# Two feed-forward products: 512-column inner products, and output sums kept in PSUM

## Chip, cores and metric

The kernel runs on one core of a Trainium2 chip. The metric is the device time of one execution in microseconds (us). In three runs the kernel before took 989.38, 989.68 and 989.70 us; 989.68 is the median.

## What is computed

The reference is one transformer layer on 512 tokens of width 1024, all in float32:

```
h = x
h = h + 0.5 * swiglu(rmsnorm(h, ffn1_norm), ffn1_w_in, ffn1_w_out)
h = h + hybrid_mixer(rmsnorm(h, mix_norm), ...)       # attention, not touched by the change
h = h + 0.5 * swiglu(rmsnorm(h, ffn2_norm), ffn2_w_in, ffn2_w_out)
out = rmsnorm(h, final_norm)

def swiglu(x, w_in, w_out):            # w_in: 1024 x 5632, w_out: 2816 x 1024
    gate, up = jnp.split(x @ w_in, 2, axis=-1)
    return (jax.nn.silu(gate) * up) @ w_out
```

The change lies in the two feed-forward parts (FFN 1 and FFN 2).

## The kernel before

**Layout.** Activations lie transposed, 128 rows of the width on the partitions and the 512 tokens along the free dimension; `h` holds eight such slices. Every float32 operand `a` of a matmul is split into a high part (rounded to the fp32r format by a ScalarE copy) and a low part (the rest, by a VectorE subtraction). A product `w x` is then three matmuls: `w_high x_high`, `w_high x_low`, `w_low x_high`.

**FFN by blocks.** The 2816 gate columns and 2816 up columns make 22 blocks of 128 + 128. Blocks 0 to 2 are plain: eight steps of three 512-column matmuls for gate and for up (lines 217 to 219). Blocks 3 to 21, the inner blocks, use a 2 x 2 scheme with seven products in place of eight: `x` is cut into upper and lower half of the width and into tokens 0 to 255 (`t1`) and 256 to 511 (`t2`), and sums of those quarters (`sums_of_x`, once per FFN) are multiplied by sums of the quarters of the weights (`sums_of_w`, once per block: lines 320 to 341). Each product has four steps of three 256-column matmuls (`product`, lines 352 to 354).

**The seven products of a block j** are issued in the order 1, (4 of block j-1), 5, 6, 2, 3, 7; 4 follows behind product 1 of the next block. Product 1 goes to `b1` (PSUM pool `sc`) and is copied to `b2` (one of two fixed banks in pool `mm`) by line 575; product 5 goes to `b3` (pool `mm`) and is copied out by line 582; product 6 adds to `b2`, and line 585 writes `b3 = b2 + su`; product 2 adds to `b1` (gate of `t1`: lines 588, 589); product 3 adds to `b3`; product 7 adds to `b2` (lines 594 to 596); product 4 adds to `b2` (gate of `t2`: lines 599, 600). `finish` (606) multiplies gate and up, and `put_g` (372, 374) splits the result. `bc` is the norm's factor, spread over all partitions.

**Output steps.** Blocks form groups that end at 2, 6, 10, 14, 18 and 22. When a group is finished, `out_steps` multiplies it by `w_out` for each of the eight slices i of `h`: the weights are split by lines 404 and 405, then 512-column matmuls (217 to 219) go into a fresh `sc` bank, and line 427, on VectorE, adds half of it to `h[i]`. These steps are spread between the inner products by `out_advance`, which pays out a budget of time after each product. The last group runs alone, in FFN 1 through `out_steps` and in FFN 2 through `out_last`.

**What sets the order.** The program states an order and a scheduler decides how each engine's queue is filled; each engine then works its own queue strictly in that order, and waits for semaphores where an operand comes from another engine. PSUM has eight banks: pool `mm` four, `sc` three, `pv` one.

Of the kernel before, what the change touches and what calls it, by code (L numbers as in the profile page):

```python
# [12 lines left out]
AF = mybir.ActivationFunctionType  # L13
ALU = mybir.AluOpType
AX = mybir.AxisListType

P = 128
T = 512
D = 1024
KB = D // P  # L20
# [13 lines left out]
ENDS = [2, 6, 10, 14, 18, 22]  # L34
# [10 lines left out]
def tile_hybrid(ctx, tc, xT, f1_wi, f1_wo, wm_t, wm_n, cw1, cw2, small, wm_oa, wm_ob, wm_oc, f2_wi, f2_wo, const, out):  # L45
# [6 lines left out]
    def f(ap):  # L52
        return ap.bitcast(F32)

    def ps(tag="mm"):
        return psp.tile([P, 512], F32, tag=tag, name=tag, bufs=NB[tag])
# [4 lines left out]
    def ps_any():  # L61
        turn[0] += 1
        return ps(wide_ps[turn[0] % 5])

    def flat(dt=F32R):
        return sb.tile([P, 1024], dt, tag="u", name="u", bufs=NU)
# [7 lines left out]
    def tmp():  # L74
        return sb.tile([P, 512], F32, tag="tmp", name="tmp", bufs=NTMP)
# [45 lines left out]
    def split_next():  # L121
        if not loaded:
            load_next()
        if loaded:
            raw, n, whole = loaded.pop(0)
            if whole:
                split.append(raw)
            else:
                wh, wl = flat(), flat()
                to_parts(raw, wh, wl, slice(0, n))  # L130
                split.append((wh, wl))
            load_next()
# [49 lines left out]
    def feed(k, gcol, xs, acc):  # L182
        parts(k, gcol, xs)
        squares(k, acc)
# [27 lines left out]
    def mm3_steps(o, wh, wl, ks, xs, first, last):  # L212
        for q, k in ks:
            c = slice(q * P, (q + 1) * P)
            s0 = first and k == ks[0][1]
            s1 = last and k == ks[-1][1]
            PE.matmul(o, wh[:, c], xs[k][:, 0, :], start=s0, stop=False)  # L217
            PE.matmul(o, wh[:, c], xs[k][:, 1, :], start=False, stop=False)  # L218
            PE.matmul(o, wl[:, c], xs[k][:, 0, :], start=False, stop=s1)  # L219
            yield 0.65  # L220

    def run(gen):
        for _ in gen:
            pass
# [7 lines left out]
    def sums_of_x(xs, gcol, XF):  # L232

        t1, t2 = slice(0, 256), slice(256, 512)
        xg = [None] * 4

        def scaled(*us):
            for u in us:
                t = xg[u] = unit(F32)
                for a in range(2):  # L240
                    k = 2 * u + a
                    gc = sm[:, gcol + k : gcol + k + 1]
                    if gcol == S_G2 and u % 2 == 0:
                        V.tensor_scalar(t[:, a, :], h[:, k, :], gc, None, op0=ALU.mult)
                    else:
                        A.activation(t[:, a, :], h[:, k, :], AF.Copy, scale=gc)

        def sums(kp, n):
            a, b = xg[kp], xg[2 + kp]
            s = flat(F32).rearrange("p (s k t) -> p s k t", s=2, k=2)  # L250
            if n == 0:
                V.tensor_tensor(s[:, 0], a[:, :, t2], b[:, :, t2], op=ALU.add)
                V.tensor_tensor(s[:, 1], s[:, 0], a[:, :, t1], op=ALU.subtract)
                s2[kp] = s[:, 1]
            else:
                V.tensor_tensor(s[:, 0], a[:, :, t1], a[:, :, t2], op=ALU.subtract)
                V.tensor_tensor(s[:, 1], b[:, :, t1], s2[kp], op=ALU.subtract)
            return s

        def high(s):  # L260
            sh = flat().rearrange("p (s k t) -> p s k t", s=2, k=2)
            A.copy(sh, s)
            return sh

        def low(s, sh, n):
            sl = flat().rearrange("p (s k t) -> p s k t", s=2, k=2)
            V.tensor_tensor(sl, s, f(sh), op=ALU.subtract)
            for m in range(2):
                XF["S", 2 * n + m + 1].extend((sh[:, m, k], sl[:, m, k]) for k in range(2))


        s2 = [None] * 2
        scaled(0)
        yield
        scaled(2)
        yield
        sa = sums(0, 0)
        yield
        scaled(1)
        sb_ = sums(0, 1)  # L280
        ha = high(sa)
        yield
        scaled(3)
        low(sa, ha, 0)
        yield
        hb = high(sb_)
        sc = sums(1, 0)
        yield
        low(sb_, hb, 1)
        sd = sums(1, 1)  # L290
        hc = high(sc)
        yield
        low(sc, hc, 0)
        hd = high(sd)
        yield
        low(sd, hd, 1)
        yield
        for name, ks, t in (("A11", 0, t1), ("A12", 4, t1), ("A22", 4, t2)):
            XF[name].extend((xs[k][:, 0, t], xs[k][:, 1, t]) for k in range(ks, ks + 4))

    def load_raw(wi, j):
        t = double()
# [43 lines left out]

    def product(o, w, x, first):

        for k in range(4):
            c = slice(k * P, (k + 1) * P)  # L350
            new = first and k == 0
            PE.matmul(o, w[0][:, c], x[k][0], start=new, stop=False, skip_group_check=not first)  # L352
            PE.matmul(o, w[0][:, c], x[k][1], start=False, stop=False, skip_group_check=not first)  # L353
            PE.matmul(o, w[1][:, c], x[k][0], start=False, stop=k == 3, skip_group_check=not first)  # L354

    def ffn(xs, acc, wi, wo, plain, gnext):

# [2 lines left out]
        bc = rcol = None  # L360
# [6 lines left out]
        nxs = []  # L367
# [50 lines left out]
            return w  # L418

        def out_steps(g):  # L420
            j0, j1 = starts[g], ENDS[g]
            last = g == len(ENDS) - 1
            for i in range(KB):
                wh, wl = out_w()
                o = ps_any() if last else ps("sc")
                yield from mm3_steps(o, wh, wl, [(q, j0 + q) for q in range(j1 - j0)], gs, True, True)
                V.scalar_tensor_tensor(h[:, i, :], o, 0.5, h[:, i, :], op0=ALU.mult, op1=ALU.add)  # L427
                if last:
                    feed(i, gnext, nxs, nacc)
                    if i == KB // 2:  # L430
                        split_next()

        def out_last():

# [63 lines left out]
        def side_step(n=1):  # L498
            for _ in range(n):
                while side and next(side[0], side) is side:  # L500
                    side.pop(0)
# [22 lines left out]
        for n in range(2 * plain):  # L524
# [30 lines left out]
            while bc is not None and held:  # L555
                gated(*held.pop(0))
        side_step(20)
        outs.append(out_steps(0))


        t1, t2 = slice(0, 256), slice(256, 512)

        banks = [ps()[:, t1] for _ in range(2)]
        for o in banks:
            PE.matmul(o, xs[0][:, 0, :P], xs[0][:, 0, t1], start=True, stop=True)

        live = {}
        later = []

        def piece_of(j, p):  # L570
            if p == 1:
                live[j] = ps("sc")[:, t1], banks[j % 2], None, None, None
                b1, b2 = live[j][:2]
                product(b1, WF.pop((j, "B11")), XF["A11"], True)
                A.copy(b2, b1)
                return
            b1, b2, b3, su, z = live[j]
            if p == 5:
                b3, su, z = ps()[:, t1], tmp(), tmp()
                live[j] = b1, b2, b3, su, z  # L580
                product(b3, WF.pop((j, "T1")), XF["S", 1], True)
                A.copy(su[:, t1], b3)
            elif p == 6:
                product(b2, WF.pop((j, "T2")), XF["S", 2], False)
                V.tensor_tensor(b3, b2, su[:, t1], op=ALU.add)
            elif p == 2:
                product(b1, WF.pop((j, "B21")), XF["A12"], False)
                V.tensor_tensor(z[:, t1], b1, bc[:, t1], op=ALU.mult)
                A.activation(z[:, t1], z[:, t1], AF.Silu)
            elif p == 3:  # L590
                product(b3, WF.pop((j, "B22")), XF["S", 4], False)
            elif p == 7:
                product(b2, WF.pop((j, "T3")), XF["S", 3], False)
                V.tensor_tensor(su[:, t2], b2, su[:, t1], op=ALU.add)
                V.tensor_tensor(su[:, t1], b3, bc[:, t1], op=ALU.mult)
                V.tensor_tensor(su[:, t2], su[:, t2], bc[:, t2], op=ALU.mult)
            elif p == 4:
                product(b2, WF.pop((j, "T4")), XF["A22"], False)
                V.tensor_tensor(z[:, t2], b2, bc[:, t2], op=ALU.mult)
                A.activation(z[:, t2], z[:, t2], AF.Silu)  # L600
                del live[j]
                later.append(finish(j, su, z))

        def finish(j, su, z):
            gg = tmp()
            V.tensor_tensor(gg, su, z, op=ALU.mult)
            yield from put_g(j, gg)

        order = []
        for j in range(plain, FB):  # L610
# [23 lines left out]
        if gnext is None:  # L634
            out_last()
        else:
            run(out_steps(len(ENDS) - 1))
        return nxs, nacc

    def last_norm(t0, sacc, sq):  # L640
# [723 lines left out]
```

## Time and profile before

| | |
|---|---|
| median of three runs | 989.68 us |
| the profiled execution | 989.41 us |
| its span, first to last instruction | 987.5 us |
| PE busy | 972.7 us |
| DVE busy | 799.8 us |
| ACT busy | 507.2 us |

PE is TensorE, PEld its weight loads, DVE VectorE, ACT ScalarE. The span is 1.9 us shorter than the execution's time. Matmuls overlap in the array, so the "mean ns" of a matmul is longer than the time at which the next one follows; what a matmul costs is the distance between the starts of two neighbours. "Idle" in a row is time of that engine alone, and costs nothing where another engine is the bottleneck.

### The profile page before, as it was taken

The page shows a single profiled execution, that of the slowest core. Times are in us where ns is not written, and L with a number is a line of the kernel's source. Part 1 is how long each engine was busy: PE and PEld are TensorE (multiplying, and loading weights), DVE is VectorE, ACT ScalarE, POOL GpSimd, SP SyncE. Part 2 cuts the span into 40 slices and gives each one's busy share as a digit, 9 for nine tenths or more (in the row PEclk, how much of TensorE's full clock was granted, in tenths as well). Part 3 has the DMA queues.
Part 4 walks back from the last instruction along what each step waited for, and adds up shares of the span by engine and source line. Part 5 has one row for each costly group of instructions (what it writes and reads, how often), then busy time and mean ns, then how long its engine had stood idle before and what let it go on. Part 6 is the DMA issues. An engine that isn't in the chain of part 4 may idle for free.

```text
span 987.5 us, 15987 instructions
## 1 busy us (share of the span) xinstructions
PE 972.7 (98%) x6228; PEld 870.4 (88%) x6228; DVE 799.8 (81%) x1459; ACT 507.2 (51%) x1037; POOL 3.8 (0%) x7
## 2 busy tenths in 40 slices
PE   9999999999999999999999999999999999999997
PEld 7889999999999889888777878889999999999996
DVE  6999788787796575788799989999978878789664
ACT  8655344353444355554678776745434435344354
POOL 0000000000000000000000000000000000000000
PEclk9999999999999999999999999999999999999999
DMA  8142413233124313123310212224231322412112
GB/s 313 44 154 102 150 44 139 76 107 131 62 86 144 125 43 106 43 71 107 130 43 8 79 44 75 86 70 162 82 136 52 130 84 99 149 44 97 45 42 86
DMA packets 36075, 93.61 MB, mean 95 GB/s; under 512 B 4384, under 2 KB 8864, under 8 KB 36000
## 3 DMA queue, kind: packets, MB, share of 16 engines
q1 hardware_dynamic: 36000, 92.59, 27.1%
q8 instruction: 49, 0.80, 0.3%
q14 instruction: 26, 0.21, 0.1%
HBM read 88.87 MB, written 2.10 MB: 92 GB/s over the span
## 4 chain that ended last, share of the span: by engine, by line
PE 91%; DVE 5%; ACT 2%; issue 1%; DMA 1%; POOL 0%; SPq 0%; DVEq 0%; ACTq 0%
PE mm L353 9%; PE mm L352 9%; PE mm L354 9%; PE sc L217 8%; PE sc L219 8%; PE sc L218 8%; PE mm L217 4%; PE mm L219 4%; PE mm L218 4%; PE sc L353 3%; PE sc L354 3%; PE sc L352 3%; PE mm L936 2%; PE pv L973 2%; PE pv L974 2%; PE mm L792 1%
## 5 line engine op out<-in xcount | busy, mean ns | idle before, releaser
L354 PE MATMUL mm<-u 128*128 128x256 f32 x760 | 214.7, 283 | 0.0
L352 PE MATMUL mm<-u 128*128 128x256 f32 x760 | 214.4, 282 | 0.3 <-ACT u L328 0.3
L353 PE MATMUL mm<-u 128*128 128x256 f32 x760 | 214.6, 282 | 0.0
L352 PEld LDWEIGHTS mm<-u 128*128 128x128 f32 x760 | 144.5, 190 | 7.7 <-ACT u L328 0.5
L353 PEld LDWEIGHTS mm<-u 128*128 128x128 f32 x760 | 144.8, 191 | 5.5
L217 PE MATMUL sc<-u 128*128 128x512 f32 x364 | 144.3, 396 | 2.3 <-ACT u L404 2.1
L354 PEld LDWEIGHTS mm<-u 128*128 128x128 f32 x760 | 144.8, 191 | 0.5
L218 PE MATMUL sc<-u 128*128 128x512 f32 x364 | 143.6, 395 | 0.0
L219 PE MATMUL sc<-u 128*128 128x512 f32 x364 | 142.7, 393 | 0.0
L217 PE MATMUL mm<-u 128*128 128x512 f32 x220 | 89.8, 408 | 0.0
L219 PE MATMUL mm<-u 128*128 128x512 f32 x220 | 86.9, 395 | 0.0
L218 PE MATMUL mm<-u 128*128 128x512 f32 x220 | 86.5, 393 | 0.0
L354 PE MATMUL sc<-u 128*128 128x256 f32 x304 | 86.0, 283 | 0.3 <-DVE u L325 0.3
L353 PE MATMUL sc<-u 128*128 128x256 f32 x304 | 85.9, 283 | 0.0
L352 PE MATMUL sc<-u 128*128 128x256 f32 x304 | 85.7, 282 | 0.0
L219 PEld LDWEIGHTS sc<-u 128*128 128x128 f32 x364 | 68.4, 188 | 17.6 <-DVE u L405 1.8
L217 PEld LDWEIGHTS sc<-u 128*128 128x128 f32 x364 | 69.2, 190 | 9.7 <-ACT u L404 2.5
L404 ACT CAST u<-tmp 128x512 fp32r<-128x512 f32 (+1 forms) x96 | 55.0, 583 | 44.2 <-PE sc L219 21.0
L218 PEld LDWEIGHTS sc<-u 128*128 128x128 f32 x364 | 69.2, 190 | 6.3
L427 DVE SCALAR_TENSOR_TENSOR h<-sc,h 128x512 f32<-128x512 f32 x85 | 58.3, 686 | 11.7 <-PE sc L219 11.6
L405 DVE TENSOR_TENSOR u<-tmp,u 128x512 fp32r<-128x512 f32 (+1 forms) x96 | 60.8, 640 | 8.2 <-ACT u L404 8.0
L352 PEld LDWEIGHTS sc<-u 128*128 128x128 f32 x304 | 57.9, 190 | 2.6
(255 smaller groups left out, 2033.7 us busy)
## 6 DMA issues: line engine op xcount, KB each, us to landing
t<-in_f_wi_dram SPq DMA_DIRECT2D x88, 512.0 KB, 4.5
tmp<-in_f_wo_dram SPq DMA_DIRECT2D x80, 256.0 KB, 4.8
t<-in_wm_t_dram SPq DMA_DIRECT2D x13, 512.0 KB, 3.8
t<-in_cw_dram SPq DMA_DIRECT2D x8, 512.0 KB, 4.5
h<-in_xT_dram SPq DMA_DIRECT2D x4, 512.0 KB, 7.4
tmp<-in_f_wo_dram SPq DMA_DIRECT2D x16, 128.0 KB, 4.6
t<-in_wm_oa_dram SPq DMA_DIRECT2D x4, 512.0 KB, 4.1
out_dram<-tmp SPq DMA_DIRECT2D x8, 256.0 KB, 2.4
```

Source lines behind the costliest of these rows:

```text
L217: PE.matmul(o, wh[:, c], xs[k][:, 0, :], start=s0, stop=False)
L218: PE.matmul(o, wh[:, c], xs[k][:, 1, :], start=False, stop=False)
L219: PE.matmul(o, wl[:, c], xs[k][:, 0, :], start=False, stop=s1)
L352: PE.matmul(o, w[0][:, c], x[k][0], start=new, stop=False, skip_group_check=not first)
L353: PE.matmul(o, w[0][:, c], x[k][1], start=False, stop=False, skip_group_check=not first)
L354: PE.matmul(o, w[1][:, c], x[k][0], start=False, stop=k == 3, skip_group_check=not first)
L404: A.copy(u[:, 0, :n], raw[:, :n])
L405: V.tensor_tensor(u[:, 1, :n], raw[:, :n], f(u[:, 0, :n]), op=ALU.subtract)
L427: V.scalar_tensor_tensor(h[:, i, :], o, 0.5, h[:, i, :], op0=ALU.mult, op1=ALU.add)
L936: PE.transpose(pt[:rows, r * P : (r + 1) * P], pl[r][:, cols], ident)
L973: PE.matmul(pv, v, u[:, 0, :], start=a, stop=False)
L974: PE.matmul(pv, v, u[:, 1, :], start=False, stop=b)
```

## The change

In `sums_of_x` the high and the low part of a sum now lie side by side in one tile, so that `u[:, :, k]` is a moving operand of 2 x 256 = 512 columns; the splits are made in pieces of 512 instead of 1024. `product` issues two matmuls per step: `w_high` by the 512 columns (high left, low right) and `w_low` by the 256 high columns, into the left half. Banks `b1`, `b2`, `b3` therefore hold two halves that must be added at the end; `joined` copies the right half out by ScalarE and adds the left half by VectorE. The two gate halves share one multiplication by `bc` and one Silu.

The output steps of groups 0 to 4 use two fixed banks `obanks` (one of `sc`, one of `pv`). ScalarE writes `2 h[i]` into the bank, the matmuls add to it, and ScalarE writes back half of the sum as `h[i]`. Line 427's addition on VectorE remains only for the last group of FFN 1 (`out_next`).

```diff
@@ -258,15 +258,15 @@
             return s
 
         def high(s):
-            sh = flat().rearrange("p (s k t) -> p s k t", s=2, k=2)
-            A.copy(sh, s)
-            return sh
-
-        def low(s, sh, n):
-            sl = flat().rearrange("p (s k t) -> p s k t", s=2, k=2)
-            V.tensor_tensor(sl, s, f(sh), op=ALU.subtract)
-            for m in range(2):
-                XF["S", 2 * n + m + 1].extend((sh[:, m, k], sl[:, m, k]) for k in range(2))
+            us = [flat().rearrange("p (a k t) -> p a k t", a=2, k=2) for _ in range(2)]
+            for m, u in enumerate(us):
+                A.copy(u[:, 0], s[:, m])
+            return us
+
+        def low(s, us, n):
+            for m, u in enumerate(us):
+                V.tensor_tensor(u[:, 1], s[:, m], f(u[:, 0]), op=ALU.subtract)
+                XF["S", 2 * n + m + 1].extend(u[:, :, k] for k in range(2))
 
 
         s2 = [None] * 2
@@ -296,7 +296,7 @@
         low(sd, hd, 1)
         yield
         for name, ks, t in (("A11", 0, t1), ("A12", 4, t1), ("A22", 4, t2)):
-            XF[name].extend((xs[k][:, 0, t], xs[k][:, 1, t]) for k in range(ks, ks + 4))
+            XF[name].extend(xs[k][:, :, t] for k in range(ks, ks + 4))
 
     def load_raw(wi, j):
         t = double()
@@ -346,12 +346,12 @@
 
     def product(o, w, x, first):
 
+
         for k in range(4):
             c = slice(k * P, (k + 1) * P)
             new = first and k == 0
-            PE.matmul(o, w[0][:, c], x[k][0], start=new, stop=False, skip_group_check=not first)
-            PE.matmul(o, w[0][:, c], x[k][1], start=False, stop=False, skip_group_check=not first)
-            PE.matmul(o, w[1][:, c], x[k][0], start=False, stop=k == 3, skip_group_check=not first)
+            PE.matmul(o, w[0][:, c], x[k], start=new, stop=False, skip_group_check=not first)
+            PE.matmul(o[:, :256], w[1][:, c], x[k][:, 0], start=False, stop=k == 3, skip_group_check=not first)
 
     def ffn(xs, acc, wi, wo, plain, gnext):
 
@@ -418,17 +418,41 @@
             return w
 
         def out_steps(g):
+
             j0, j1 = starts[g], ENDS[g]
-            last = g == len(ENDS) - 1
+
+            def seed(i):
+                A.activation(obanks[i % 2], h[:, i, :], AF.Copy, scale=2.0)
+
+            if g == 0:
+                seed(0)
             for i in range(KB):
                 wh, wl = out_w()
-                o = ps_any() if last else ps("sc")
-                yield from mm3_steps(o, wh, wl, [(q, j0 + q) for q in range(j1 - j0)], gs, True, True)
+                o = obanks[i % 2]
+                if i + 1 < KB:
+                    seed(i + 1)
+                for q in range(j1 - j0):
+                    c = slice(q * P, (q + 1) * P)
+                    u = gs[j0 + q]
+                    PE.matmul(o, wh[:, c], u[:, 0, :], start=False, stop=False, skip_group_check=True)
+                    PE.matmul(o, wh[:, c], u[:, 1, :], start=False, stop=False, skip_group_check=True)
+                    PE.matmul(o, wl[:, c], u[:, 0, :], start=False, stop=q == j1 - j0 - 1, skip_group_check=True)
+                    yield 0.65
+                A.activation(h[:, i, :], o, AF.Copy, scale=0.5)
+                if i == KB - 1 and g < len(ENDS) - 2:
+                    seed(0)
+
+        def out_next():
+
+            j0, j1 = starts[-1], ENDS[-1]
+            for i in range(KB):
+                wh, wl = out_w()
+                o = ps_any()
+                run(mm3_steps(o, wh, wl, [(q, j0 + q) for q in range(j1 - j0)], gs, True, True))
                 V.scalar_tensor_tensor(h[:, i, :], o, 0.5, h[:, i, :], op0=ALU.mult, op1=ALU.add)
-                if last:
-                    feed(i, gnext, nxs, nacc)
-                    if i == KB // 2:
-                        split_next()
+                feed(i, gnext, nxs, nacc)
+                if i == KB // 2:
+                    split_next()
 
         def out_last():
 
@@ -555,56 +579,66 @@
             while bc is not None and held:
                 gated(*held.pop(0))
         side_step(20)
+        obanks = [ps("sc"), ps("pv")]
+        for o in obanks:
+            PE.matmul(o, xs[0][:, 0, :P], xs[0][:, 0, :], start=True, stop=True)
         outs.append(out_steps(0))
 
 
         t1, t2 = slice(0, 256), slice(256, 512)
 
-        banks = [ps()[:, t1] for _ in range(2)]
+        banks = [ps() for _ in range(2)]
         for o in banks:
-            PE.matmul(o, xs[0][:, 0, :P], xs[0][:, 0, t1], start=True, stop=True)
+            PE.matmul(o, xs[0][:, 0, :P], xs[0][:, 0, :], start=True, stop=True)
 
         live = {}
         later = []
 
+        def joined(z, o):
+
+            A.copy(z, o[:, t2])
+            V.tensor_tensor(z, o[:, t1], z, op=ALU.add)
+
         def piece_of(j, p):
             if p == 1:
-                live[j] = ps("sc")[:, t1], banks[j % 2], None, None, None
+                live[j] = ps("sc"), banks[j % 2], None, None, None
                 b1, b2 = live[j][:2]
                 product(b1, WF.pop((j, "B11")), XF["A11"], True)
                 A.copy(b2, b1)
                 return
             b1, b2, b3, su, z = live[j]
             if p == 5:
-                b3, su, z = ps()[:, t1], tmp(), tmp()
+                b3, su, z = ps(), tmp(), tmp()
                 live[j] = b1, b2, b3, su, z
                 product(b3, WF.pop((j, "T1")), XF["S", 1], True)
-                A.copy(su[:, t1], b3)
+                A.copy(su, b3)
             elif p == 6:
                 product(b2, WF.pop((j, "T2")), XF["S", 2], False)
-                V.tensor_tensor(b3, b2, su[:, t1], op=ALU.add)
+                V.tensor_tensor(b3, b2, su, op=ALU.add)
             elif p == 2:
                 product(b1, WF.pop((j, "B21")), XF["A12"], False)
-                V.tensor_tensor(z[:, t1], b1, bc[:, t1], op=ALU.mult)
-                A.activation(z[:, t1], z[:, t1], AF.Silu)
+                joined(z[:, t1], b1)
             elif p == 3:
                 product(b3, WF.pop((j, "B22")), XF["S", 4], False)
             elif p == 7:
                 product(b2, WF.pop((j, "T3")), XF["S", 3], False)
-                V.tensor_tensor(su[:, t2], b2, su[:, t1], op=ALU.add)
-                V.tensor_tensor(su[:, t1], b3, bc[:, t1], op=ALU.mult)
-                V.tensor_tensor(su[:, t2], su[:, t2], bc[:, t2], op=ALU.mult)
+                V.tensor_tensor(su, b2, su, op=ALU.add)
+                w = tmp()
+                joined(w[:, t1], b3)
+                V.tensor_tensor(w[:, t2], su[:, t1], su[:, t2], op=ALU.add)
+                V.tensor_tensor(w, w, bc, op=ALU.mult)
+                live[j] = b1, b2, b3, w, z
             elif p == 4:
                 product(b2, WF.pop((j, "T4")), XF["A22"], False)
-                V.tensor_tensor(z[:, t2], b2, bc[:, t2], op=ALU.mult)
-                A.activation(z[:, t2], z[:, t2], AF.Silu)
+                joined(z[:, t2], b2)
+                V.tensor_tensor(z, z, bc, op=ALU.mult)
+                A.activation(z, z, AF.Silu)
                 del live[j]
                 later.append(finish(j, su, z))
 
         def finish(j, su, z):
-            gg = tmp()
-            V.tensor_tensor(gg, su, z, op=ALU.mult)
-            yield from put_g(j, gg)
+            V.tensor_tensor(su, su, z, op=ALU.mult)
+            yield from put_g(j, su)
 
         order = []
         for j in range(plain, FB):
@@ -634,7 +668,7 @@
         if gnext is None:
             out_last()
         else:
-            run(out_steps(len(ENDS) - 1))
+            out_next()
         return nxs, nacc
 
     def last_norm(t0, sacc, sq):
```

**On TensorE**, at block 10 of FFN 1: the last step of product 2 (tile `sc_1572`, after the change `sc_1420`) and the first output step behind it. Before:

```order
L352 MATMUL sc_1572<-u_131,u_1503 128x256
L353 MATMUL sc_1572<-u_131,u_1503 128x256
L354 MATMUL sc_1572<-u_131,u_1504 128x256
L217 MATMUL sc_1657<-u_1474,u_1446 128x512
L218 MATMUL sc_1657<-u_1474,u_1446 128x512
L219 MATMUL sc_1657<-u_1474,u_1446 128x512
```

After the change:

```order
L353 MATMUL sc_1420<-u_131,u_1363 128x512
L354 MATMUL sc_1420<-u_131,u_1364 128x256
L437 MATMUL sc_458<-u_1338,u_1314 128x512
L438 MATMUL sc_458<-u_1338,u_1314 128x512
L439 MATMUL sc_458<-u_1338,u_1314 128x512
```

Of the step's three matmuls two are left, the first of them of 512 columns; the output step keeps its three and goes to the fixed bank `sc_458`.

**On VectorE**, at the same block, around the sum `b3 = b2 + su` behind product 6 (line 585, after the change 617). Before:

```order
L606 TENSOR_TENSOR tmp_1604<-tmp_1485,tmp_1486 128x512
L374 TENSOR_TENSOR u_1606<-tmp_1604,u_1606 128x512
L585 TENSOR_TENSOR mm_1613<-mm_450,tmp_1614 128x256
L331 TENSOR_TENSOR u_1611<-t8_1586,u_1610 128x1024
L336 TENSOR_TENSOR u_1633<-t8_1378,u_1632 128x1024
L588 TENSOR_TENSOR tmp_1615<-sc_1572,bc_321 128x256
```

After the change:

```order
L640 TENSOR_TENSOR tmp_1415<-tmp_1415,tmp_1350 128x512
L617 TENSOR_TENSOR mm_1454<-mm_462,tmp_1455 128x512
L374 TENSOR_TENSOR u_1447<-tmp_1415,u_1447 128x512
L331 TENSOR_TENSOR u_1452<-t8_1430,u_1451 128x1024
L600 TENSOR_TENSOR tmp_1456<-sc_1420,tmp_1456 128x256
L336 TENSOR_TENSOR u_1470<-t8_1255,u_1469 128x1024
```

The sum stands in the same place of the queue, directly behind the product of gate and up of the block before, and is twice as wide. Line 588 (gate times `bc`) has become line 600 (the addition of the two halves).

**On ScalarE**, at block 11, where the weights of the block and of the output steps are split. Before:

```order
L328 CAST u_1610<-t8_1586 128x1024
L334 CAST u_1632<-t8_1378 128x1024
L339 CAST u_1649<-t8_1586 128x1024
L404 CAST u_1652<-tmp_1385 128x512
L589 ACTIVATE tmp_1615<-tmp_1615 128x256
L404 CAST u_1701<-tmp_1449 128x512
```

After the change:

```order
L328 CAST u_1589<-t8_1565 128x1024
L404 CAST u_1593<-tmp_1488 128x512
L441 ACTIVATE h_61<-sc_458 128x512
L334 CAST u_1620<-t8_1395 128x1024
L425 ACTIVATE sc_458<-h_61 128x512
L339 CAST u_1636<-t8_1565 128x1024
L599 COPY tmp_1607<-sc_1555 128x256
```

Lines 441 (half of the bank to `h`) and 425 (`2 h` into the bank) have come between the splits, and line 599 (the copy of the right half out of `b1`).

## Rows read from the trace of the kernel before

**Rows 1.** The page, parts 1, 2: busy us (share) xinstructions; clock in tenths.
```profile
PE 972.7 (98%) x6228; PEld 870.4 (88%) x6228; DVE 799.8 (81%) x1459; ACT 507.2 (51%) x1037; POOL 3.8 (0%) x7
PEclk9999999999999999999999999999999999999999
```

**Rows 2.** The page, part 4: shares of the chain that ended last.
```profile
PE 91%; DVE 5%; ACT 2%; issue 1%; DMA 1%; POOL 0%; SPq 0%; DVEq 0%; ACTq 0%
```

**Rows 3.** Windows: us; busy of PE, PEld, DVE, ACT, POOL; clock; DMA.
```profile
24.00:52.00 28.00, 25.85 (x142) 21.97 (x140) 26.65 (x36) 16.52 (x25) 1.57 (x1) 1.00 0.19 66
76.00:335.00 259.00, 259.00 (x1806) 241.55 (x1806) 204.87 (x315) 110.05 (x182) 0.00 (x0) 1.00 0.30 106
660.00:684.00 24.00, 23.62 (x167) 22.02 (x166) 23.29 (x39) 12.90 (x24) 0.00 (x0) 1.00 0.42 144
```

**Rows 4.** Timeline of PE: start us, us, what. 256 columns, 60 matmuls.
```profile
205.84 0.28 PE L352 MATMUL mm<-u 128*128 128x256 f32 x1
...
208.71 0.28 PE L352 MATMUL mm<-u 128*128 128x256 f32 x1
...
212.91 0.28 PE L354 MATMUL sc<-u 128*128 128x256 f32 x1
```

**Rows 5.** Timeline of PE, 512 columns only, 60 matmuls.
```profile
336.05 0.39 PE L217 MATMUL sc<-u 128*128 128x512 f32 x1
...
349.43 0.39 PE L219 MATMUL sc<-u 128*128 128x512 f32 x1
```

**Rows 6.** Timeline of PE, an output step between 256-column products.
```profile
203.02 0.40 PE L217 MATMUL sc<-u 128*128 128x512 f32 x1
203.25 0.40 PE L218 MATMUL sc<-u 128*128 128x512 f32 x1
203.49 0.39 PE L219 MATMUL sc<-u 128*128 128x512 f32 x1
203.72 0.28 PE L352 MATMUL mm<-u 128*128 128x256 f32 x1
203.83 0.28 PE L353 MATMUL mm<-u 128*128 128x256 f32 x1
```

**Rows 7.** Groups by line and shape: count | busy us, mean ns | idle.
```profile
L352 PE MATMUL mm<-u 128*128 128x256 f32 x760 | 214.4, 282 | 0.3 <-ACT u L328 0.3
L352 PE MATMUL sc<-u 128*128 128x256 f32 x304 | 85.7, 282 | 0.0
L427 DVE SCALAR_TENSOR_TENSOR h<-sc,h 128x512 f32<-128x512 f32 x85 | 58.3, 686 | 11.7 <-PE sc L219 11.6
L606 DVE TENSOR_TENSOR tmp<-tmp 128x512 f32<-128x512 f32 x38 | 26.2, 689 | 10.6 <-ACT tmp L600 10.6
L267 DVE TENSOR_TENSOR u<-u 128x1024 fp32r<-128x1024 f32 x8 | 9.8, 1221 | 0.1
L585 DVE TENSOR_TENSOR mm<-mm,tmp 128x256 f32<-128x256 f32 x38 | 16.3, 428 | 0.7
L246 ACT ACTIVATE u<-h,sm 128x512 f32<-128x512 f32 x12 | 7.9, 717 | 0.0
L944 ACT COPY tmp<-pv 64x512 f32<-64x512 f32 x16 | 9.3, 584 | 7.7 <-PE pv L974 7.3
L582 ACT COPY tmp<-mm 128x256 f32<-128x256 f32 x38 | 13.9, 365 | 6.1 <-PE mm L354 6.1
```

**Rows 8.** The same view, 76 to 335 us alone.
```profile
L427 DVE SCALAR_TENSOR_TENSOR h<-sc,h 128x512 f32<-128x512 f32 x32 | 22.0, 686 | 5.1 <-PE sc L219 5.1
L585 DVE TENSOR_TENSOR mm<-mm,tmp 128x256 f32<-128x256 f32 x17 | 7.3, 428 | 0.3
```

**Rows 9.** Timeline of DVE around the sum behind product 6.
```profile
206.77 1.22 DVE L331 TENSOR_TENSOR u<-t,u 128x1024 fp32r<-128x1024 f32 x1
207.90 0.43 DVE L585 TENSOR_TENSOR mm<-mm,tmp 128x256 f32<-128x256 f32 x1
```

**Rows 10.** PE waits, 24 to 76 us: total us, times, longest.
```profile
PE sc L217 <- ACT u L404: 1.7, 1, 1.7
```

## Prediction

> **What bounds the kernel now.** I read the page's busy times first. TensorE is busy for 972.7 of 987.5 us, VectorE for 799.8, ScalarE for 507.2, and the granted clock is full in every slice, the 2.4 GHz level [rows 1]. A busy share can hide idle array time, so the chain that ended last comes second: PE carries 91% of it, DVE 5% [rows 2]. Third, the windows by stage: between 76 and 335 us, inside FFN 1's inner blocks, PE is busy for all of 259.00 us, DVE for 204.87 (79%) and ACT for 110.05 (42%) [rows 3]. There only what changes the spacing of matmuls, or makes PE wait, changes the time. At the start of the inner blocks it is closer: DVE is busy for 26.65 of 28 us before 52 us and for 23.29 of 24 us between 660 and 684 us [rows 3], and PE once waits 1.7 us for ScalarE's split of output weights [rows 10].
>
> A matmul's duration does not tell what it costs, since the next one starts before it ends. So the fourth view is the timeline, read for starts. Sixty 256-column matmuls start between 205.84 and 212.91 us: 7.07 / 59 = 0.1198 us each [rows 4]. Sixty 512-column ones start between 336.05 and 349.43 us: 13.38 / 59 = 0.2268 us each [rows 5]. Twice the columns thus cost 0.107 us more, which leaves some 0.013 us in every matmul that does not depend on its width. The change removes one such part per step.
>
> **The matmuls.** Line 352 stands for 760 + 304 = 1064 steps [rows 7], the same count as the seven products of 19 blocks in two FFNs with four steps each. A step costs 3 x 0.1198 = 0.3595 us now. Afterwards it is one 512 and one 256, in turn. The trace has no such alternation, so I bound it:
> - the 512 as in a stretch of its own kind: 0.2268 + 0.1198 = 0.3466, gain 0.0129 per step, 13.7 us in all;
> - the slowest neighbour shown, a second 512 behind a 256 (203.25 to 203.49, 0.24): 0.36 per step, gain zero;
> - the kindest pairing, a 512 directly behind a 256 (203.02 to 203.25, 0.23) and a 256 directly behind a 512 (203.72 to 203.83, 0.11): 0.34, gain 0.02, 21 us [rows 6].
>
> I take 0.23 + 0.12 = 0.35: the 512 from the row that is nearest to the new pattern, the 256 from the long stretch, since 0.11 is a single distance of two decimals. Gain 0.0095 x 1064 = 10.1 us. That the 512 columns lie in two pieces of 256 I cost at nothing: the instruction reads as many elements. If reading in pieces costs time, the bound of zero gain covers it.
>
> How much of a matmul is fixed is also stated by the Trainium skill, "TensorE: Matmul & The Clock Gate", section "Back-to-back issue gap": with a warm array an isolated matmul follows after its columns divided by 2.4 GHz plus 2.5 ns. By that rule a merged step gains 2.5 ns, 2.7 us in all instead of 10.1. The trace disagrees with it: 0.1198 us for 256 columns is 13 ns above 256 / 2.4 GHz, and 0.2268 us is 13 ns above 512 / 2.4 GHz [rows 4, 5].
>
> **Banks at the start.** Before, two 256-column matmuls per FFN open banks (line 565); now four of 512 do (584, 592). 8 x 0.227 - 4 x 0.120 = +1.3 us, or nothing if they fall into a wait such as the 1.7 us [rows 10]. I charge 1.3.
>
> **The DVE-bound starts.** The splits of the sums, eight 1024-wide subtractions of 1221 ns, become sixteen of 512 at about 689 [rows 7]: per FFN 8 x 0.689 - 4 x 1.221 = +0.6 us, and the first inner block adds 1.9 us (below). Nothing is late if DVE's remaining idle time takes it, up to 2.5 us per FFN if all of it shows; as line 427's work goes away there, up to the 1.7 us wait may also be gained. I take 0.8 each, the splits and a little, since the block's own extra comes behind its first products: +1.6 us.
>
> **VectorE inside the blocks.** Priced with 0.428 us for 256 columns and 0.689 for 512 [rows 7]: the sums behind products 6 and 7 double (+0.26 each); the gate of `t1` trades its multiplication for the joining addition (0); the gate of `t2` gains a 512-wide multiplication (+0.69); the up part has two 256 and one 512 in place of two 256 (+0.69). That is +1.9 us per block. Line 427 leaves, 0.686 per slice. Over 76 to 335 us there are 17 blocks and 32 slices [rows 8]: +32.3 - 22.0 = +10.3, so 215 us of what will be some 255: 84%. It fits.
>
> **ScalarE.** Two copies grow from 256 to 512 (0.365 to 0.584), three copies of 0.365 are new, the Silu I leave as it is: +1.53 per block. Each slice adds a seed and a write-back, 0.584 to 0.717 each [rows 7]. 17 x 1.53 + 64 x 0.65 = +68 on 110 us [rows 3, 8]: 70%. It fits too. For the output steps' new waits the cover is the second bank: a bank's twelve matmuls of a four-block group take 12 x 0.23 = 2.8 us, while write-back and seed of the other take 1.3 plus one weight split ahead of them. Behind a write-back that waits for PE stand the weight splits of the next block; they have most of a block (259 / 17 = 15 us [rows 3, 8]) until they are used. I charge nothing; if the cover goes, it is the last rival's loss.
>
> **Ends of the FFNs.** The last gate now runs through copy, join, multiplication, Silu, product and split: 0.37 + 0.43 + 0.69 + 0.6 + 0.69 + 0.6 = 3.4 us by the rows of its kinds [rows 7]. On PE, fourteen output matmuls of the group before and nine of the last group stand ahead of the first that needs it, 23 x 0.227 = 5.2 us [rows 5]. Cost nothing.
>
> **Sum.** From the profiled execution, 989.41 us (span 987.5 and 1.9 around it): - 10.1 + 1.3 + 1.6 = 982.2. The median of the runs is 0.3 above that execution, so 982.5 us.
>
> **Rivals.**
> 1. All of it shows. The alternation costs 0.3466 and the starts hide their extra: 989.7 - 13.7 = 976.0. For it speaks that both widths show the same 13 ns; against it that 512s behind 256s run slower than 512s alone, 0.70 us per three instead of 0.68 [rows 5, 6].
> 2. Switching widths costs what merging saves: 0.355 to 0.36 per step, a gain of 0 to 5 us against 2.9 of extra, so 987.6 to 992.6, middle 989.9. For it speaks the 0.24 [rows 6]; against it that the fixed part is alike in both stretches, and that the 256 directly behind a 512 comes early. The page's 2.5 ns would end at the same place, 989.9.
> 3. Slower: product 3 waits for the sum behind product 6. Now the sum starts at 207.90 behind a 1.22 us operation, ends at 208.33, and product 3's first matmul starts at 208.71: 0.38 spare [rows 4, 9]. The sum gets 0.26 longer and product 2 some 0.04 shorter, which leaves 0.08. The order of VectorE puts the 512-wide product of gate and up directly ahead of it, and that one waits for a Silu on ScalarE, which in turn waits for a longer join. If that makes the sum 0.69 late in half of the 38 blocks, PE loses 19 x 0.61 = 11.6 us: 994.1. It outweighs the gain of 7.2 us from 0.19 us per block. Against it: 16% of VectorE stays free, and output steps stand between products in most blocks, 0.7 us of other matmuls each.
>
> **Chances.** The forecast 0.52 (its own range 979.5 to 985.5), rival 1 0.13, rival 2 0.17, rival 3 0.18. What this measurement can tell from no change is about 0.2%, 2.0 us, that is 987.7 and 991.7. Faster: 0.52 + 0.13 + 0.04 of rival 2 = 0.69. Same: 0.09 of rival 2 and 0.03 of rival 3 = 0.12. Slower: 0.04 + 0.15 = 0.19. The range reaches from the dearer half of rival 1 to the middle of rival 2's upper half: 977 to 991.5; the rest of rival 3 and the best of rival 1 lie outside.
>
> **What the new profile would show.** Lines 353 and 354 with 1064 matmuls each; starts 0.35 us apart per step (0.3466 for rival 1, 0.355 and more for rival 2); a full PE inside the blocks with DVE near 84% and ACT near 70%. In the list of waits, PE on line 353 released by DVE line 617 or 625 would be rival 3, by ACT line 425 a failure of the two banks. A wait at the first output step well over 1.7 us would show the starts under-priced. The forecast is wrong if the steps are 0.35 and the total is not near 982, since then PE waits somewhere that I costed at nothing.

## The result, and the profile after

The changed kernel takes 978.84 us (median of 4 runs, 978.62 to 978.95) against 989.58 before in the same comparison (989.38 to 989.7): ratio 0.9891, interval 0.9874 to 0.9909. The forecast was 982.5, range 977 to 991.5: the time lies inside, on the fast side, 3.7 us under the forecast. The profiled execution has a span of 976.8 us, 10.7 less than before.

The page of the kernel after, parts 1, 2 and 4 (columns as in [rows 1, 2]):

```profile
PE 963.3 (99%) x5168; PEld 814.2 (83%) x5168; DVE 816.8 (84%) x1463; ACT 634.5 (65%) x1281; POOL 3.6 (0%) x7
...
PEclk9999999999999999999999999999999999999999
...
PE 95%; DVE 2%; ACT 1%; DMA 0%; issue 0%; POOL 0%; SPq 0%; DVEq 0%; ACTq 0%
```

Instructions on PE are 1060 fewer: 1064 merged, four openers more. The clock is the 2.4 GHz level throughout, as before. DVE's share of the chain fell from 5% to 2% [rows 2].

The windows after, of stretches that answer to [rows 3]:

```profile
24.00:52.00 28.00, 26.56 (x128) 21.62 (x128) 25.53 (x37) 18.77 (x32) 1.37 (x1) 1.00 0.20 56
76.00:332.00 256.00, 256.00 (x1337) 217.43 (x1336) 216.25 (x320) 164.31 (x283) 0.00 (x0) 1.00 0.32 110
655.00:679.00 24.00, 24.00 (x128) 20.51 (x127) 22.11 (x34) 19.02 (x36) 0.00 (x0) 1.00 0.41 143
```

Inside the blocks PE is full again, DVE is at 84% (forecast 84%), ACT at 64% (forecast 70%). At both starts (FFN 2 now begins 5 us earlier) VectorE is busy for about 1.1 us less than before, not more. In FFN 1 that is no relief: between 24 and 52 us its splits of the sums rose from 4.9 to 5.4 us as charged, but it stands idle for 2.0 us for ScalarE's line 372 (see below). In FFN 2 four additions of line 427 (2.7 us) have left the window.

Starts of the merged products, timeline of PE after (product 6 on `mm`, then product 2 on `sc`, then product 3):

```profile
202.34 0.39 PE L353 MATMUL mm<-u 128*128 128x512 f32 x1
202.56 0.28 PE L354 MATMUL mm<-u 128*128 128x256 f32 x1
202.68 0.40 PE L353 MATMUL mm<-u 128*128 128x512 f32 x1
...
203.74 0.40 PE L353 MATMUL sc<-u 128*128 128x512 f32 x1
...
205.15 0.40 PE L353 MATMUL mm<-u 128*128 128x512 f32 x1
```

Eight steps take 205.15 - 202.34 = 2.81 us, 0.351 each; before it was 0.3595 [rows 4].

The sum behind product 6 in the same place, timeline of DVE:

```profile
204.28 0.69 DVE L617 TENSOR_TENSOR mm<-mm,tmp 128x512 f32<-128x512 f32 x1
204.88 1.22 DVE L331 TENSOR_TENSOR u<-t,u 128x1024 fp32r<-128x1024 f32 x1
```

It ends at 204.97, and product 3 starts at 205.15: 0.18 us spare of the 0.38 before [rows 9].

Groups after, by line and shape, against [rows 7]:

```profile
L353 PE MATMUL mm<-u 128*128 128x512 f32 x760 | 273.5, 396 | 0.0
L353 PE MATMUL sc<-u 128*128 128x512 f32 x304 | 110.6, 396 | 1.1 <-ACT u L322 1.1
L425 ACT ACTIVATE sc<-h 128x512 f32<-128x512 f32 x40 | 24.1, 603 | 3.8 <-PE sc L584 3.3
L441 ACT ACTIVATE h<-sc 128x512 f32<-128x512 f32 x40 | 23.9, 597 | 6.0 <-PE sc L439 5.8
L268 DVE TENSOR_TENSOR u<-u 128x512 fp32r<-128x512 f32 x16 | 10.6, 689 | 0.0
```

Where the 10.64 us of span went. Each row adds distances between starts of neighbouring matmuls; what a distance has over 0.25 us is counted as a wait:

| place | before, us | after, us | difference |
|---|---|---|---|
| up to the first inner matmul of FFN 1 | 43.42 | 44.78 | +1.36 |
| inner matmuls of both FFNs, waits taken off | 382.69 | 372.52 | -10.17 |
| the waits in them | 2.80 | 1.20 | -1.60 |
| output-step matmuls between them | 194.61 | 193.92 | -0.69 |
| between the two inner stretches (FFN 2's openers in it) | 326.14 | 326.65 | +0.51 |
| after them | 37.83 | 37.78 | -0.05 |

The step is 372.52 / 1064 = 0.3501 us: the term that carries the forecast came out as written. What it missed lies at the start of FFN 1. Waits of PE, 24 to 76 us, after (total us, times, longest); the 1.7 us of [rows 10] is gone, another is there:

```profile
PE sc L353 <- ACT u L322: 1.1, 1, 1.1
PE sc L354 <- DVE u L325: 0.3, 1, 0.3
```

ScalarE just before it, timeline of ACT after (start, us; in brackets the idle time ahead and what ended it):

```profile
39.15 0.63 ACT L381 ACTIVATE tmp<-tmp 128x512 f32<-128x512 f32 x1
43.07 0.60 ACT L425 ACTIVATE sc<-h 128x512 f32<-128x512 f32 x1 [3.29 <-PE sc L584]
43.61 0.60 ACT L372 CAST u<-tmp 128x512 fp32r<-128x512 f32 x1
44.11 0.62 ACT L322 CAST u<-t 128x512 fp32r<-128x512 f32 x1
```

The first seed (425) waits 3.29 us for a bank's opener (584), which stands on PE behind the last plain matmul. The weight split (322) that the first inner product needs is queued behind that seed.

### The profile page after: what moved, and what is told of

Its sections match the earlier page's. It is cut to its first block, busy times and chain, and to the rows that moved or that the text cites. A ratio compares the mean times of both kernels' runs of the same rounds, so it can differ in the third digit from the quotient of the medians.

```text
span 976.8 us, 13986 instructions
## 1 busy us (share of the span) xinstructions
PE 963.3 (99%) x5168; PEld 814.2 (83%) x5168; DVE 816.8 (84%) x1463; ACT 634.5 (65%) x1281; POOL 3.6 (0%) x7
## 4 chain that ended last, share of the span: by engine, by line
PE 95%; DVE 2%; ACT 1%; DMA 0%; issue 0%; POOL 0%; SPq 0%; DVEq 0%; ACTq 0%
PE mm L353 18%; PE mm L354 9%; PE sc L353 7%; PE mm L217 5%; PE mm L219 5%; PE mm L218 5%; PE sc L354 4%; PE pv L437 3%; PE pv L439 3%; PE sc L438 3%; PE sc L437 3%; PE pv L438 3%; PE sc L439 3%; PE mm L970 2%; PE sc L217 2%; PE sc L219 2%
## 5 line engine op out<-in xcount | busy, mean ns | idle before, releaser
L353 PE MATMUL mm<-u 128*128 128x512 f32 x760 | 273.5, 396 | 0.0
L354 PE MATMUL mm<-u 128*128 128x256 f32 x760 | 211.4, 279 | 0.1
L353 PEld LDWEIGHTS mm<-u 128*128 128x128 f32 x760 | 142.6, 188 | 33.8 <-DVE tmp L625 0.8
L354 PEld LDWEIGHTS mm<-u 128*128 128x128 f32 x760 | 143.2, 188 | 6.4 <-DVE u L331 0.4
L353 PE MATMUL sc<-u 128*128 128x512 f32 x304 | 110.6, 396 | 1.1 <-ACT u L322 1.1
L217 PE MATMUL mm<-u 128*128 128x512 f32 x220 | 89.8, 408 | 0.0
L219 PE MATMUL mm<-u 128*128 128x512 f32 x220 | 86.9, 395 | 0.0
L218 PE MATMUL mm<-u 128*128 128x512 f32 x220 | 86.5, 393 | 0.0
L354 PE MATMUL sc<-u 128*128 128x256 f32 x304 | 85.0, 280 | 0.3 <-DVE u L325 0.3
L353 PEld LDWEIGHTS sc<-u 128*128 128x128 f32 x304 | 57.1, 188 | 14.7 <-ACT u L322 1.5
L404 ACT CAST u<-tmp 128x512 fp32r<-128x512 f32 (+1 forms) x96 | 54.7, 582 | 18.7 <-PE sc L439 13.6
L599 ACT COPY tmp<-mm 128x256 f32<-128x256 f32 x76 | 28.3, 372 | 50.7 <-PE mm L354 50.7
L354 PEld LDWEIGHTS sc<-u 128*128 128x128 f32 x304 | 57.2, 188 | 3.5 <-DVE u L325 0.6
L437 PE MATMUL pv<-u 128*128 128x512 f32 x144 | 57.2, 397 | 0.0
L437 PE MATMUL sc<-u 128*128 128x512 f32 x144 | 56.8, 394 | 0.0
L438 PE MATMUL sc<-u 128*128 128x512 f32 x144 | 56.8, 394 | 0.0
L439 PE MATMUL pv<-u 128*128 128x512 f32 x144 | 56.8, 394 | 0.0
L438 PE MATMUL pv<-u 128*128 128x512 f32 x144 | 56.6, 393 | 0.0
L439 PE MATMUL sc<-u 128*128 128x512 f32 x144 | 56.2, 390 | 0.0
L331 DVE TENSOR_TENSOR u<-t,u 128x1024 fp32r<-128x1024 f32 x38 | 46.4, 1222 | 4.8 <-ACT u L328 2.8
L219 PEld LDWEIGHTS mm<-u 128*128 128x128 f32 x220 | 41.3, 188 | 8.5 <-DVE u L106 0.2
```

Source lines behind the costliest of these rows:

```text
L331: V.tensor_tensor(wl, t[:, 0:1024], f(wh), op=ALU.subtract)
L353: PE.matmul(o, w[0][:, c], x[k], start=new, stop=False, skip_group_check=not first)
L354: PE.matmul(o[:, :256], w[1][:, c], x[k][:, 0], start=False, stop=k == 3, skip_group_check=not first)
L404: A.copy(u[:, 0, :n], raw[:, :n])
L437: PE.matmul(o, wh[:, c], u[:, 0, :], start=False, stop=False, skip_group_check=True)
L438: PE.matmul(o, wh[:, c], u[:, 1, :], start=False, stop=False, skip_group_check=True)
```

## Experiments

**Theory**: merging gains a fixed part of each matmul, 0.0095 us per step; the output part gains little itself and frees VectorE. **Rivals**: the gain comes from the output steps; a step of 512 and 256 columns is cheap for another reason than the count; widths in turn cost something still.

**Merging alone.** Output steps as before, and without the two openers of `obanks` ("..." stands for lines left out):

```diff
-                o = obanks[i % 2]
-                ...
-                A.activation(h[:, i, :], o, AF.Copy, scale=0.5)
+                o = ps_any() if last else ps("sc")
+                yield from mm3_steps(o, wh, wl, ...)
+                V.scalar_tensor_tensor(h[:, i, :], o, 0.5, h[:, i, :], op0=ALU.mult, op1=ALU.add)
```

> The merged inner products alone; output steps add on VectorE as in the kernel before. Theory (each matmul has a fixed part of some 0.013 us, and 1064 of them are gone): 979 to 981 us, inner steps 0.350 us as in the changed kernel. Rival (the output sums in PSUM are what makes it possible): VectorE then carries 204.9 + 32.3 = 237 of 255 us inside the blocks, 93%, and PE waits for the sums behind products 6 and 7: 984 to 990 us.

Measured 981.85 us (981.7 to 981.94), ratio 0.9921, interval 0.9907 to 0.9934: nearer the theory, but 0.85 us over its range. The inner matmuls without waits take 373.02 us, nearly the 372.52 after, so the step is as the theory has it; yet 3.0 us of the whole change's gain are missing. They lie in the output steps: their distances over 0.25 us add up to 4.2 us instead of 0.8, while the missing openers and seeds give 1.4 us back at the first start. The window and the waits of PE (52 to 345 us) of this kernel:

```profile
76.00:332.00 256.00, 254.68 (x1331) 216.02 (x1330) 232.85 (x354) 130.50 (x217) 0.00 (x0) 1.00 0.32 110
```

```profile
PE sc L217 <- ACT u L372: 1.3, 1, 1.3
PE mm L353 <- DVE mm L590: 0.6, 1, 0.6
PE sc L217 <- ACT u L404: 0.4, 1, 0.4
```

VectorE is at 91%, and PE waits for its work. The 1.3 us happen once in each FFN; the first, in the timelines of DVE, ACT and PE in turn:

```profile
92.60 0.69 DVE L607 TENSOR_TENSOR tmp<-tmp,bc 128x512 f32<-128x512 f32 x1
93.20 0.68 DVE L325 TENSOR_TENSOR u<-t,u 128x512 fp32r<-128x512 f32 x1
93.80 0.69 DVE L330 TENSOR_TENSOR t<-t,t 128x512 f32<-128x512 f32 x1
94.41 0.68 DVE L613 TENSOR_TENSOR tmp<-tmp 128x512 f32<-128x512 f32 x1
```

```profile
95.12 0.62 ACT L372 CAST u<-tmp 128x512 fp32r<-128x512 f32 x1 [0.88 <-DVE tmp L613]
```

```profile
95.80 0.50 PE L217 MATMUL sc<-u 128*128 128x512 f32 x1 [1.32 <-ACT u L372]
```

VectorE goes from one operation to the next without a gap, so the gate of a block (607, 613) and its split (372) come too late for the first output step that needs them. The 0.6 us for line 590 is rival 3's mechanism, a product that waits for the sum behind product 6, with a fuller VectorE.

**The output part alone.** Products of 256 columns, output sums in PSUM (`product`, `high`, `low` and `piece_of` as before).

> The output sums in PSUM alone; inner products of three 256-column matmuls as before. Theory: PE was full inside the blocks, so only the openers of two banks (+0.9) and the output steps' spacing (0.2319 instead of 0.2333, -0.7 in both FFNs) and some of the 1.7 us wait at the first output step change: 987.5 to 990 us. Rival (the output sums carry a share of the gain of their own): 986 us or less.

Measured 988.63 us (988.26 to 989.3), ratio 0.9989, interval 0.998 to 0.9998: theory. Its window:

```profile
76.00:335.00 259.00, 259.00 (x1805) 241.64 (x1805) 186.22 (x280) 143.43 (x247) 0.00 (x0) 1.00 0.31 108
```

VectorE drops from 79% to 72% and PE gains nothing inside the blocks: 18.7 us of an engine that is off the path. The gain is the waits, 2.80 to 1.22 us in the inner stretches; at the two starts 0.8 us of it is lost again, where the openers are new. So -7.8 (merging, within its comparison) and -1.1 (outputs) add to -8.9, and both give -10.7: the output part is worth more where merging has filled VectorE.

**The merged product issued as two matmuls of 256**, everything else as after:

```diff
-            PE.matmul(o, w[0][:, c], x[k], ...)
+            PE.matmul(o[:, :256], w[0][:, c], x[k][:, 0], ...)
+            PE.matmul(o[:, 256:], w[0][:, c], x[k][:, 1], ...)
```

> The changed kernel with the 512-column matmul of each inner step issued as two of 256 columns, everything else of the change kept (high and low side by side, two halves joined, output sums in PSUM). Theory of the fixed part per matmul: the whole gain of the products goes back, 978.8 + 10.2 = 989 us, steps of 0.359 us. Rival (the layout, the wider banks or the fewer changes of bank carry the gain): 979 to 983 us.

Measured 990.88 us (990.63 to 991.22), ratio 1.0013, interval 1.0004 to 1.0022: theory, some 2 us over it. Timeline of PE, one step:

```profile
204.03 0.28 PE L353 MATMUL mm<-u 128*128 128x256 f32 x1
204.15 0.28 PE L354 MATMUL mm<-u 128*128 128x256 f32 x1
204.26 0.28 PE L355 MATMUL mm<-u 128*128 128x256 f32 x1
204.38 0.28 PE L353 MATMUL mm<-u 128*128 128x256 f32 x1
```

The inner matmuls take 382.32 us, 9.8 more than after, for 1064 more matmuls over the same columns: 9.2 ns each. The gain is the count, not the layout or the joins. Another 2.6 us come in the output steps' matmuls (196.56 against 193.92), which this edit does not touch; 1.3 of them are distances over 0.25 us, and why they grow is open.

**Grouped by width.** Per product four matmuls of 512, then four of 256; the same count:

```diff
         for k in range(4):
             PE.matmul(o, w[0][:, c], x[k], ...)
+        for k in range(4):
+            c = slice(k * P, (k + 1) * P)
             PE.matmul(o[:, :256], w[1][:, c], x[k][:, 0], ...)
```

> The changed kernel with the four 512-column matmuls of a product issued first and its four 256-column ones behind them: two changes of width per product instead of eight, the same count. Theory (only the count matters): 978 to 979.6 us. Rival (each change of width costs a few ns, which is why a step takes 0.3504 us and not 0.3466): 3 of 4 changes gone, up to 0.0038 x 1064 x 3/4 = 3 us less, 975.8 to 977 us.

Measured 976.95 us (976.79 to 977.03), ratio 0.9871, interval 0.9858 to 0.9885: the rival; counting alone does not explain it. Timeline of PE:

```profile
202.05 1.08 PE L353 MATMUL mm<-u 128*128 128x512 f32 x4
202.97 0.64 PE L356 MATMUL mm<-u 128*128 128x256 f32 x4
203.44 1.09 PE L353 MATMUL sc<-u 128*128 128x512 f32 x4
204.37 0.64 PE L356 MATMUL sc<-u 128*128 128x256 f32 x4
204.85 1.09 PE L353 MATMUL mm<-u 128*128 128x512 f32 x4
```

The inner matmuls take 370.45 us, 0.3482 per step, 2.1 us less than after. Between 76 and 330 us a 512 takes 0.2303 us ahead of another and 0.2274 ahead of a 256; in turns it takes 0.2338. A 256 takes 0.1163 in turns and 0.1177 or 0.1211 grouped. So turns cost the 512 more than they save on the 256. It goes with the place in a run of 512s: in this window of the grouped kernel the first two of a run take 0.233 and 0.235 us, the sixth 0.227. In the kernel before, where all 512s of the window are output steps with the moving operand in one piece, the first two take 0.235 as well, so the two pieces of the merged operand are not needed to explain it.

**The first seed freed from its wait.** One bank (`pv`) is opened inside the last plain product and serves the even output steps; the other is opened where both were (not shown):

```diff
                 for k, _ in enumerate(mm3_steps(o, wh, wl, ALLK, xs, True, True)):
                     between(n, k)
+                    if n == 2 * plain - 1 and k == 5:
+                        obanks = [ps("pv")]
+                        PE.matmul(obanks[0], ..., start=True, stop=True)
```

> The changed kernel with one edit: the bank pv is opened inside the last plain product (after its step 5) and is the bank of the even output steps, so that ScalarE's first seed (line 425) no longer waits for an opener behind the last plain matmul. In the changed kernel ScalarE waits there 3.29 us for PE line 584, with the splits of the last plain block (372) and of the first inner block's weights (322) queued behind it, and PE then waits 1.07 us for line 322. Theory (the seed's place in ScalarE's queue made the first inner matmul late, not the splits of the sums and not the openers' own time): ScalarE takes up line 372 at about 41.7 us instead of 43.61, the 1.07 us wait goes, the first inner matmul starts at 43.5 to 43.8 us instead of 44.78, 977.7 to 978.0 us in all. Rival A (the later subtractions on VectorE set the start): the wait stays at about 1 us, released by line 325 or 322, 978.5 to 979.0. Rival B (the start is earlier, but the wait for the output weights of line 404, 1.7 us before the change, comes back): 978.6 to 979.6.

Measured 977.37 us (977.1 to 977.76), ratio 0.9878, interval 0.9861 to 0.9894: theory, 0.3 us under its range, and neither rival. ACT, then PE, in their timelines:

```profile
41.91 0.60 ACT L425 ACTIVATE pv<-h 128x512 f32<-128x512 f32 x1 [1.93 <-PE pv L572]
42.45 0.60 ACT L372 CAST u<-tmp 128x512 fp32r<-128x512 f32 x1
42.96 0.62 ACT L322 CAST u<-t 128x512 fp32r<-128x512 f32 x1
```

```profile
43.76 0.40 PE L353 MATMUL sc<-u 128*128 128x512 f32 x1
44.44 0.38 PE L354 MATMUL sc<-u 128*128 128x256 f32 x1 [0.28 <-DVE u L325]
```

The seed still waits, but it is served 1.16 us earlier; the first inner matmul comes at 43.76 instead of 44.78 and follows the openers directly. Of the +1.36 in the table, 1.03 was the seed's place in ScalarE's queue. The span is 975.5 us, 1.4 less than after; most of the other 0.4 lies in the inner stretch of FFN 1 (284.03 instead of 284.29 us from its first matmul to its last).

**Grouped and opened early**, the two edits together.

> The grouped order (per product four 512-column matmuls, then four of 256) together with the early opener of pv. Theory (the two gains lie in different places and add): 976.95 less 0.8 to 1.1, that is 975.8 to 976.2 us. Rival (an earlier start only moves the wait to the output weights): 976.7 to 977.5.

Measured 975.73 us (975.38 to 976.01), ratio 0.986, interval 0.9845 to 0.9875: they add (1.2 us less than grouped alone, a little more than expected). This is the fastest version, ahead of the changed kernel and of the one before.

**The low weights' product as two of 128 columns.** Twice the narrow matmuls, the same columns and weights:

```diff
-            PE.matmul(o[:, :256], w[1][:, c], x[k][:, 0], ...)
+            PE.matmul(o[:, P:256], w[1][:, c], x[k][:, 0, P:256], ...)
+            PE.matmul(o[:, :P], w[1][:, c], x[k][:, 0, :P], ...)
```

> The changed kernel with the product of the low weights (256 columns) issued as two of 128 columns with the same weights: 1064 matmuls more, the same columns. Theory (each matmul carries a fixed part of 13 ns whatever its width): 978.8 + 1064 x 0.013 = 992.7 us, 991 to 995. Rival (a matmul cannot be shorter than the load of its 128 x 128 weights; 128-wide transposes of this kernel start about 0.109 us apart): a pair costs 0.218 instead of 0.12, 978.8 + 1064 x 0.098 = 1083 us, 1070 to 1090. It tells whether the narrow matmul of 256 columns can be cut further and whether the fixed part can be carried to narrower ones.

Measured 1105.34 us (1104.38 to 1106.08), ratio 1.1169, interval 1.1153 to 1.1186: the theory's 13 ns fail here, and even the rival's range ends 15 us short. Timeline of PE, one step:

```profile
206.47 0.45 PE L353 MATMUL mm<-u 128*128 128x512 f32 x1
206.76 0.22 PE L354 MATMUL mm<-u 128*128 128x128 f32 x1
206.82 0.27 PE L355 MATMUL mm<-u 128*128 128x128 f32 x1
206.93 0.45 PE L353 MATMUL mm<-u 128*128 128x512 f32 x1
```

The weight loads of the same step, timeline of PEld:

```profile
206.31 0.19 PEld L355 LDWEIGHTS mm<-u 128*128 128x128 f32 x1
206.41 0.19 PEld L353 LDWEIGHTS mm<-u 128*128 128x128 f32 x1
206.53 0.19 PEld L354 LDWEIGHTS mm<-u 128*128 128x128 f32 x1
```

A step is 0.46 us instead of 0.35: about 0.11 more for one more matmul over the same columns, so 117 of the 126 us. The groups of this kernel put another 9.3 us of PE's idle time down to the sum behind product 6. A small fixed part holds between 256 and 512 columns; the two of 128 gained nothing by being narrower. The loads behind the narrow pair start 0.11 us apart (medians 0.108 and 0.111), though the two narrow matmuls themselves start 0.06 us apart. Half of the 0.11 us is paid by the pair (0.058 + 0.112 against 0.116 for the one), half by the 512 behind it (0.286 against 0.234). That the load of the weights sets this limit fits these rows and the 0.109 us of the transposes, but no run varied the load by itself.

## Why the prediction was right, and where it was off

- **The matmuls** (-10.1): right in the sum, -10.17 measured, step 0.3501 against 0.35. Of its parts, the 512 was taken a little too cheap (0.23 for 0.2338) and the 256 too dear (0.12 for 0.1163). Merging alone and splitting again both confirm that it is the count. The rule that the Trainium skill gives for an isolated matmul ("TensorE: Matmul & The Clock Gate", section "Back-to-back issue gap"), by which 2.7 us were to be had, does not carry over to this kernel: the 9.2 ns per added matmul of the split version stand against its 2.5.
- **Banks at the start** (+1.3): in FFN 2 the time from the first opener to the first inner matmul went from 0.24 to 0.90 us, +0.66, as charged. In FFN 1 they stand on the path too once the wait behind them is gone.
- **The DVE-bound starts** (+1.6): this step failed, in cause and sign. The splits grew as charged, 0.5 us on VectorE, but do not reach the path: with the seed freed, the first inner product follows the openers directly and the one wait for VectorE, 0.28 us for line 325, stood in the kernel before as well. In their place stand a wait not forecast, 1.03 us by the seed's place in ScalarE's queue, and a gain that I had named but not booked, the 1.7 us of [rows 10]. The output part alone removes that wait too; with merging alone 0.4 of it stay. Both starts and the waits together cost 1.36 + 0.51 - 1.60 = +0.27 us where I had charged 2.9. The prediction's last sign, steps of 0.35 and a total not near 982, thus came true the other way round: not a wait that I had costed at nothing, but waits charged that did not come.
- **The output steps** (0): 0.69 us faster, not forecast. This and the line above make most of the 3.7 us; what shortens them is open.
- **VectorE and ScalarE inside the blocks**: no wait of PE inside the blocks, DVE as forecast. ScalarE was overpriced, +54 us for the +68 of the sum: a seed or write-back takes 0.60 us, not 0.65, and the two Silus of 256 columns became one of 512. The larger part is that neighbouring operations overlap (the first seed starts at 43.07 and lasts 0.60 us, the next operation starts at 43.61): the durations in the window rise by 62.3 us, the busy time by 54.3. That the outputs' work leaves VectorE is what keeps it so: with merging alone PE loses 1.3 us per FFN to a late gate. **Ends of the FFNs** (0): no wait of PE there, right.
- **Rivals**: 1 did not show in the step (0.3501, not 0.3466), though the gap to it is partly the turns of widths; its other half, starts that hide their extra, nearly came true (+0.27 us); 2 was wrong, with a true core that is worth 2 us and not 10 (the middle of its 987.6 to 992.6 is 990.1, not 989.9); 3 did not happen, the sum had 0.18 us to spare in the block shown, where I had left 0.08, and no wait for line 617 stands in the list of PE's waits.

## What to carry to other kernels

Where PE is full, price a merge of matmuls by starts, not durations, in stretches of both widths, and then group equal widths if order is free. Price a part that relieves another engine by what the rest of the change puts on that engine: alone it was worth 1.1 us here, together 3. For each new instruction that waits on PE, ask what stands behind it in its own queue, above all at the start of a stage, where a wait of a cheap operation holds up the weights of the next one.

## What the runs showed of the hardware that I had not expected

- The distance between matmuls depends on the widths around them: 512 columns took 0.2338 us in turns with 256, 0.2303 among their own kind in products, 0.2268 in long stretches alone [rows 5]. The first two 512s behind narrower ones are the slow ones (0.233 to 0.235).
- Halving 256 columns to two of 128 saved nothing: the pair, with the matmul behind it, cost about 0.11 us more than the one.
- The same output-step matmuls took 194.6, 193.9, 196.6 and 194.6 us (before, after, two of 256, grouped) with products of other shapes between them; only part of that is waiting.
